# Token tiles are turned whole and kept in SBUF, with ScalarE rounding each chunk and VectorE forming its full value beside it

## The chip, the core and the metric

The kernel runs on one core of one Trainium2 chip. The metric is the time of one execution on the device in microseconds (us); the median of three runs before the change is 723.25 us (721.90 to 723.26). TensorE is also called PE, VectorE DVE, ScalarE ACT and GpSimd POOL; SyncE (SP) issues most of the DMA transfers.

## What is computed

One layer of a hybrid attention block is applied to 128 prompt tokens and 1,024 latent tokens, nine tiles of 128 tokens with 1,024 features. The part that matters here is its beginning, cut from the reference:

```python
shift, scale, gate = modulation(c, w_mod[l], b_mod[l])        # silu(c) @ w_mod + b_mod, in thirds
h = rmsnorm(xs, norm_gain[l]) * (1.0 + scale) + shift
p = h @ w_in                                                  # queries, keys, values and gates of two head groups
...
xs = xs + gate * merge_out(o_a, g_a, o_b, g_b, w_out[l])      # (o_a * silu(g_a), o_b * silu(g_b)) @ w_out
```

The prompt tokens get the same with `c_ctx` in place of `c`. So a token has to be normalized (squares summed over its features), scaled and shifted per feature, and then multiplied with the weights. Global and windowed attention, the output projection and the residual follow; the change does not touch them.

## The kernel before

**Precision.** A product of two float32 matrices is made of three TensorE products in a faster format (fp32r). Each operand is split into a rounded part (high) and the remainder (low): high x high, high x low and low x high are summed in PSUM. For the weights `Weights.split` does that (L229): ScalarE casts the high part, VectorE subtracts (`whi`, `wlo`). For the tokens it is done once in the opening stage: `h_at(0, ...)` is the high part, `h_at(1, ...)` the low one.

**Layout.** Products contract over features, so tokens must lie with the features on partitions: tile t (`xn[t]`, 128 tokens x 1,024 features) is turned in eight blocks of 128x128, one for each chunk k of 128 features, by TensorE transposes into PSUM. Scale and shift are then one number per partition (`a_mod`, `b_col`). The nine tiles stand in the order 1 to 8, then 0 (the prompt), and are cut in thirds: tiles 1 to 4 (512 columns), 5 and 6 (256), 7, 8 and 0 (384).

**The opening stage** (L333 to L502) makes `h` chunk by chunk and, at the same time, the first gate projection `W_GA` of the first two thirds. In pass j of the loop at L441:

- `W_GA.split` splits chunk j of the weights, and loads a later one;
- `first_gates(ch, j-1)` adds chunk j-1 of 512 tokens to four PSUM banks `big[0..3]`, `next_gates(ch, j-2)` that of 256 tokens to `small`;
- `modulate_rows(j)` multiplies `silu(c)` with chunk j of the modulation weights `wm` (1 MB a chunk); `modulate(j)` turns the result, and VectorE makes `a_mod` and `b_col` of chunk j from it (a reduce and two small operations, L361 to L365);
- `transposed(j, 1, 4, 0)` and `transposed(j, 5, 2, 0)` turn chunk j of four and of two tiles into a PSUM bank `px`. From there ScalarE applies scale and shift (`hf`, L401), VectorE rounds that to the high part (L406), and GpSimd subtracts for the low part (L407). From pass 5 on, `more` does the same for tiles 7, 8 and 0.

So each chunk of each tile takes the way PE, ScalarE, VectorE, GpSimd inside the pass before the one in which its products are issued.

Ahead of it, `norm(t)` (L378) makes a tile's norm: ScalarE squares and sums it (L382), GpSimd makes the inverse root (L384, L386), and VectorE scales the tile in place (`scaled`, L376). Tiles 1 to 6 are normalized in pass 0, tiles 7, 8 and 0 in passes 2 to 4. `warm` (L417) issues bfloat16 products whose result nobody reads, 24 in all before the first gate product.

**Order.** The program's order is each engine's order: `in_order` (L93) chains the instructions of an engine as they were written, and SP issues its DMAs in that order too. A tile's buffer is taken again when its last reader is done. A DMA that has to wait for a buffer holds back those behind it on SP.

After the loop `put_gates` applies silu to a bank and writes it to DRAM (scheduled for later ticks but for the first one), and `gates(W_GA, 0, W_QA, THIRDS[2:])` makes the last third. Its first PSUM bank is one of the two of `big[0]` and `big[1]`.

Of the kernel before, what the change touches and what calls it, by code (L numbers as in the profile page):

```python
# [18 lines left out]
P = 128  # L19
D = 1024  # L20
# [36 lines left out]
X_FROM = 1  # L57
SECOND_FROM = 5
WARM = (8, 4, 4, 2)
WIDE = 5  # L60
# [47 lines left out]
def hybrid_step(ctx, tc, x_prompt, x_sample, cache_k_a, cache_v_a, cache_k_b, cache_v_b,  # L108
# [97 lines left out]
    class Weights:  # L206
# [22 lines left out]
        def split(self):  # L229
# [4 lines left out]
            eng = nc.gpsimd if self.tag in POOL_LO and k % 2 else nc.vector  # L234
            eng.tensor_tensor(l, self.raw[k], h, op=ALU.subtract)
            self.hi.append(h)
            self.lo.append(l)
            self.load()
# [72 lines left out]
    with tc.tile_pool(name="st", bufs=2, side="right") as st:  # L311
# [16 lines left out]
        def load_wm(j):  # L328
            w = st.tile([P, KT, 2, P], F32, tag="wm", name=f"wm{j}", bufs=3)
            nc.sync.dma_start(w, w_mod_ss[j])  # L330
            wm.append(w)

        load_wm(0)  # L333
# [12 lines left out]
        def modulate_rows(j):  # L346
# [6 lines left out]
            (nc.scalar.copy if j else nc.vector.tensor_copy)(mrows[j], pm[:, 0:256])  # L353
# [13 lines left out]
        xn = {}  # L367
# [5 lines left out]
        rx = {}  # L373

        def scaled(t, r):
            nc.vector.tensor_scalar(xn[t], xn[t], r, None, op0=ALU.mult)  # L376

        def norm(t, now_=True):  # L378
            xm = xn[t]
            sq = st.tile([P, D], BF16, tag="sq", name=f"sq{t}", bufs=1)  # L380
            ss = st.tile([P, 1], F32, tag="ss", name=f"ss{t}")
            nc.scalar.activation(sq, xm, AF.Square, accum_out=ss)  # L382
            ms = st.tile([P, 1], F32, tag="ms", name=f"msx{t}")
            nc.gpsimd.tensor_scalar(ms, ss, 1.0 / D, EPS, op0=ALU.mult, op1=ALU.add)  # L384
            r = st.tile([P, 1], F32, tag="rs", name=f"rsx{t}")
            nc.gpsimd.tensor_tensor(r, ms, mhalf[:, 0:1], op=ALU.pow)  # L386
            if now_:
                scaled(t, r)
            else:
                rx[t] = r  # L390

        def transposed(j, t0, n, cond):
            px = bank_tr(f"px{j}_{t0}")
            for i in range(n):
                if j == 0 and t0 == 1:
                    warm(WARM[3])
                nc.tensor.transpose(px[:, P * i : P * i + P], xn[t0 + i][:, P * j : P * j + P], ident)
            w = P * n
            dst = slice(P * place(t0), P * place(t0) + w)
            hf = st.tile([P, 512], F32, tag="hf", name=f"hf{j}_{t0}", bufs=3)  # L400
            nc.scalar.activation(hf[:, :w], px[:, :w], AF.Identity,  # L401
                                 scale=a_mod[:, j, cond : cond + 1], bias=b_col[:, j, cond : cond + 1])
            step = w if third(dst) else 2 * P
            for o in range(0, w, step):
                i, to = third(slice(dst.start + o, dst.start + o + step))
                nc.vector.tensor_copy(h_at(0, i, j, to), hf[:, o : o + step])  # L406
                nc.gpsimd.tensor_tensor(h_at(1, i, j, to), hf[:, o : o + step], h_at(0, i, j, to), op=ALU.subtract)  # L407

        for t in FIRST[:4]:
            load_x(t)  # L410
        W_GA.load()
        load_x(5)
        load_x(6)
        load_wm(1)
        W_GA.load()
        load_wm(2)
        def warm(n):  # L417

            for _ in range(n):
                nc.tensor.matmul(small[0], ident_b, ident_b.unsqueeze(1).to_broadcast([P, 4, P]), start=True, stop=True)  # L420

        rest = [7, 8, 0]
        second = [(j, 7, 2, 0) for j in range(WIDE)] + [(j, 0, 1, 1) for j in range(KT)]

        big = [bank("AABB"[ch], f"pg0_{ch}_f") for ch in range(4)]
        small = [bank("C", f"pg0_{ch}_s") for ch in (0, 2)]
# [8 lines left out]
        def more():  # L435
            ready = [x for x in second if x[0] <= j]
            if ready and j >= SECOND_FROM:
                second.remove(ready[0])
                transposed(*ready[0])

        for j in range(KT + 2):  # L441
            if j == 0:
                warm(WARM[0])
                norm(1)
                modulate_rows(0)
                warm(WARM[1])
                norm(2)
                modulate(0)
                warm(WARM[2])
                norm(3)  # L450
                norm(4)
                W_GA.split()
                norm(5)
                transposed(0, 1, 4, 0)
                norm(6)
                load_wm(3)
                continue
            big_on, small_on = j <= KT, 2 <= j
            if j < KT:
                W_GA.split()  # L460
            if big_on:
                first_gates(0, j - 1, 0)
                first_gates(1, j - 1, 0)
            if j < KT:
# [3 lines left out]
                if X_FROM <= j < X_FROM + 3:  # L468
                    load_x(rest[j - X_FROM])
# [3 lines left out]
            if j == 1:  # L473
                transposed(0, 5, 2, 0)
            if big_on:
# [6 lines left out]
            if j < KT:  # L482
                transposed(j, 5, 2 if j < WIDE else 4, 0)
            if X_FROM + 1 < j <= X_FROM + 4:
                t = rest[j - X_FROM - 2]
                scaled(t, rx.pop(t))
            if X_FROM < j <= X_FROM + 3:
# [835 lines left out]
```

## Time and profile before

| | |
|---|---|
| median of three runs | 723.25 us (721.90, 723.25, 723.26) |
| span of the profiled execution | 721.3 us |
| its own time | one of the three above; 0.6 to 2.0 us lie around the span |
| mean granted TensorE clock | 0.993 |
| PE, PEld, DVE, ACT, POOL busy | 97%, 78%, 63%, 57%, 46% of the span |
| first gate product (L262) | at 17.47 us |
| second, third, fourth pass begin | at 25.30, 31.69, 37.99 us |
| first product of the last third | at 72.53 us |
| DMA | 78.56 MB in all |

The span runs from the first to the last instruction. Rows of the timeline give start and duration in us, engine, line and operation, output <- input, and in brackets how long the engine was idle before it and what released it. Rows of the windows give for a stretch its length, then each engine's busy time with the number of instructions, the granted TensorE clock (1.00 is full), the share of the DMA engines' time and GB/s. Rows of groups give the total busy time and the mean in ns.

### The profile page before, as it was taken

What the parts mean: (1) busy time and instruction counts of PE and PEld (TensorE: products, weight loads), DVE (VectorE), ACT (ScalarE), POOL (GpSimd) and SP (SyncE); (2) the same over time, 40 slices, a digit from 0 to 9 for tenths busy, and PEclk for the clock granted to TensorE, in tenths of its full rate; (3) what the DMA queues carried; (4) which work ended last, traced back from release to release, by engine and by line L of the source; (5) the groups of instructions that cost most, each with busy time, mean ns of one, the idle gap of its engine ahead of it and who ended that gap; (6) DMA issues with size and microseconds to landing.
All of it is one profiled execution on the core that took longest, in us unless ns stands there. A gap on an engine that the chain in (4) does not pass through costs nothing. (4 is left out here: it accounts for less than half of the span.)

```text
span 721.3 us, 10622 instructions
## 1 busy us (share of the span) xinstructions
PE 698.3 (97%) x3524; PEld 559.7 (78%) x3524; DVE 457.6 (63%) x1007; ACT 411.7 (57%) x829; POOL 335.3 (46%) x355
## 2 busy tenths in 40 slices
PE   5999999999999999999999999999999999999997
PEld 2678988877777788977788888888888888887865
DVE  3466147875675872745866677577666775775653
ACT  5355411411232451158778877877787778877770
POOL 3456013332322340236666555655575557555751
PEclk9999999999999999999999999999999999999999
DMA  8961373348435115440321222121212221212323
GB/s 344 346 219 59 121 278 86 79 94 276 121 85 142 45 60 171 139 143 23 103 67 45 73 67 88 44 81 52 87 54 59 66 87 45 81 53 87 103 65 119
DMA packets 53159, 78.56 MB, mean 109 GB/s; under 512 B 6569, under 2 KB 25449, under 8 KB 52081
## 3 DMA queue, kind: packets, MB, share of 16 engines
q1 hardware_dynamic: 44928, 65.96, 28.1%
q10 hardware_dynamic: 8176, 11.94, 6.3%
q8 instruction: 28, 0.46, 0.3%
q14 instruction: 27, 0.21, 0.1%
HBM read 58.69 MB, written 19.18 MB: 108 GB/s over the span
## 5 line engine op out<-in xcount | busy, mean ns | idle before, releaser
L1108 POOL TENSOR_TENSOR pl<-pe,ph 128x512 fp32r<-128x512 f32 x130 | 167.6, 1292 | 144.7 <-DVE nm L919 67.5
L859 DVE TENSOR_REDUCE mx<-pmx 128x1 f32<-128x384 f32 x192 | 101.4, 552 | 59.5 <-PE pmx L858 58.1
L1100 ACT ACTIVATE pe<-st 128x512 f32<-128x512 f32 x146 | 86.8, 594 | 28.0 <-PE st L1098 27.1
L1104 ACT CAST ph<-pe 128x512 fp32r<-128x512 f32 x146 | 90.6, 621 | 4.8
L1118 PE MATMUL pv<-ph,v_hi 128*128 128x512 f32 x208 | 83.2, 400 | 2.2 <-DVE spare L1142 2.2
L1121 PE MATMUL pv<-pl,v_hi 128*128 128x512 f32 x208 | 82.6, 397 | 0.0
L173 POOL TENSOR_TENSOR rs_q<-ms_q,mhalf 128x8 f32<-128x8 f32 x18 | 34.8, 1931 | 82.1 <-DVE ms_q L171 82.1
L1189 PE MATMUL po<-wo,ogh 128*128 128x512 f32 x216 | 72.5, 394 | 0.2 <-DVE yt L1196 0.2
L919 DVE CUSTOM_DVE_ANT_0 sn<-sn,mask,nsink 128x512 f32<-128x512 f32 (+1 forms) x64 | 46.3, 724 | 38.3 <-PE sn L916 36.5
L858 PE MATMUL pmx<-kha,qt 128*128 128x384 f32 x192 | 61.0, 363 | 0.4 <-ACT pen L905 0.2
L1097 PE MATMUL st<-qt,kha 128*128 128x512 f32 x144 | 58.3, 405 | 1.5 <-ACT pe L1100 0.8
L1098 PE MATMUL st<-qb,kla 68*128 68x512 f32 x144 | 57.6, 400 | 1.1 <-DVE qb L878 1.1
L1120 PE MATMUL pv<-ph,v_lo 128*64 128x512 f32 x146 | 57.9, 396 | 0.0
L1121 PEld LDWEIGHTS pv<-pl,v_hi 128*128 128x128 f32 x208 | 39.4, 189 | 16.7 <-issue 0.2
L905 ACT ACTIVATE pen<-sn,nm 128x512 f32<-128x512 f32 (+2 forms) x72 | 45.0, 626 | 6.5 <-DVE nm L919 3.1
L1093 ACT CAST ph<-st 128x512 fp32r<-128x512 f32 x62 | 36.4, 587 | 19.9 <-PE st L1092 18.7
L1118 PEld LDWEIGHTS pv<-ph,v_hi 128*128 128x128 f32 x208 | 39.4, 189 | 10.5 <-ACT ogh L1154 2.4
L1189 PEld LDWEIGHTS po<-wo,ogh 128*128 128x128 f32 x216 | 40.0, 188 | 6.8 <-DVE yt L1196 0.6
L1094 DVE TENSOR_TENSOR pl<-st,ph 128x512 fp32r<-128x512 f32 x62 | 42.5, 686 | 2.3 <-ACT ph L1093 1.5
L1189 PE MATMUL po<-wo,ogl 128*128 128x512 f32 x108 | 42.6, 394 | 0.0
L594 ACT ACTIVATE sqq<-pq 128x512 f32<-128x512 f32 x18 | 10.8, 599 | 53.3 <-DMA qd<-qo0q 14.4
L858 PEld LDWEIGHTS pmx<-kha,qt 128*128 128x128 f32 x192 | 35.5, 190 | 6.2 <-DVE mx L859 1.4
(216 smaller groups left out, 1700.2 us busy)
## 6 DMA issues: line engine op xcount, KB each, us to landing
qt<-qd SPq DMA_DIRECT2D x36, 256.0 KB, 3.1
wm<-in_w_mod_ss_dram SPq DMA_DIRECT2D x8, 1024.0 KB, 5.1
qd<-qo0q ACTq DMA_DIRECT2D x36, 128.0 KB, 2.4
qd<-qo1q ACTq DMA_DIRECT2D x36, 128.0 KB, 2.4
sgl<-gd SPq DMA_DIRECT2D x36, 128.0 KB, 2.1
out_dram<-yt SPq DMA_DIRECT2D x17, 256.0 KB, 2.1
xn<-in_x_sample_dram SPq DMA_DIRECT2D x8, 512.0 KB, 7.0
wg<-in_w_mod_g_dram SPq DMA_DIRECT2D x4, 1024.0 KB, 7.9
```

The source lines that it names most:

```text
L858: nc.tensor.matmul(pm[:, 0:384], lhs, kha[:, g, 3 * b : 3 * b + 3, :], start=True, stop=True)
L859: nc.vector.tensor_reduce(mx[:, h, b : b + 1], pm[:, 0:384], axis=AX.X, op=ALU.max)
L919: nc.vector.tensor_tensor_reduce(s, s, mask[:, m0 : m0 + n], -1.0, nsink[:, 4 * g + h : 4 * g + h + 1], op0=ALU.add, op1=ALU.min, accum_ou ...
L1097: nc.tensor.matmul(s, kh, qtile[i], start=True, stop=False)
L1098: nc.tensor.matmul(s, kl, qbtile[i], start=False, stop=True)
L1100: nc.scalar.activation(pe, s, AF.Exp)
L1104: nc.scalar.copy(ph, pe)
L1108: nc.gpsimd.tensor_tensor(pl, pe, ph, op=ALU.subtract)
L1118: nc.tensor.matmul(pv, two, ph, start=(b == 0), stop=False)
L1120: nc.tensor.matmul(pv[0:64, :], vl, ph, start=False, stop=False)
L1121: nc.tensor.matmul(pv, two, pl, start=False, stop=last)
L1189: nc.tensor.matmul(po[n], a, wo_parts[KT * n + k][lo], start=(k == KS[0] and p == 0), stop=(k == KS[-1] and p == 2))
```

## The change

The opening stage is written in another way; nothing else changes.

- **Loads.** Tiles 1 to 4 come first on SP's queue, then `wm0` in two halves, then the first weight chunk, tile 5, `wm1`, tile 6, and so on. Before, `wm0` came first. Token tiles share four buffers, so the load of tile 5 waits until tile 1 is turned, 6 for 2, 7 for 3, 8 for 4, 0 for 5.
- **Turning.** `turned_tile(t)` turns all eight blocks of a tile into two banks, and `keep` copies them from PSUM to a new SBUF tile `xT` (1,024 features x 1,152 tokens), one bank by ScalarE and one by VectorE. Tiles 1 to 4 are turned before the first gate product, 5 in pass 1, 6 in pass 2, and 7, 8, 0 in passes 3, 4, 5.
- **Modulating.** `modulated` reads `xT`: ScalarE writes the high part straight from it (scale, shift and rounding in one), VectorE makes the full value `hf` from the same input, and GpSimd subtracts as before. The high part of a chunk no longer goes through VectorE.
- **Squares.** The squares of tiles 1 to 4 stand first in ScalarE's queue; those of 5 to 0 are spread over the passes.
- Warm products: 8 at the start and 4 before the first gate product. The low part of the first weight chunk is made by GpSimd. `mrows` of chunk 1 is copied by VectorE. The first `put_gates` stands before the last pass, and `sg` has two buffers of its own (before it shared three with `hf`). `more` starts at the same pass, but makes up to four pieces a pass.

```diff
-WARM = (8, 4, 4, 2)
-WIDE = 5
+WARM = (8, 4)
...
-        load_wm(0)
         nc.scalar.activation(silc, colt[:, 0:16], AF.Silu)
...
-            (nc.scalar.copy if j else nc.vector.tensor_copy)(mrows[j], pm[:, 0:256])
+            (nc.scalar.copy if j > 1 else nc.vector.tensor_copy)(mrows[j], pm[:, 0:256])
...
+        xT = st.tile([P, KT, TOK], F32, name="xT", bufs=1)
 
         def load_x(t):
-            xn[t] = st.tile([P, D], F32, name=f"xn{t}", bufs=1)
+            xn[t] = st.tile([P, D], F32, tag="xn", name=f"xn{t}", bufs=4)
             nc.sync.dma_start(xn[t], x_tile[t])
...
+        def turned_tile(t, tags, between=None):
+
+            for c in range(2):
+                if c and between:
+                    between()
+                px[t, c] = bank(tags[c], f"px{t}_{c}")
+                for i in range(4):
+                    k = 4 * c + i
+                    nc.tensor.transpose(px[t, c][:, P * i : P * i + P], xn[t][:, P * k : P * k + P], ident)
+
+        def keep(t, c, copy):
+            at = slice(P * place(t), P * place(t) + P)
+            copy(xT[:, 4 * c : 4 * c + 4, at], px.pop((t, c)).rearrange("p (k n) -> p k n", n=P))
+
+        def modulated(j, t0, n, cond):
...
+            a, b = (x[:, j, cond : cond + 1] for x in (a_mod, b_col))
             hf = st.tile([P, 512], F32, tag="hf", name=f"hf{j}_{t0}", bufs=3)
-            nc.scalar.activation(hf[:, :w], px[:, :w], AF.Identity,
-                                 scale=a_mod[:, j, cond : cond + 1], bias=b_col[:, j, cond : cond + 1])
-            step = w if third(dst) else 2 * P
-            for o in range(0, w, step):
-                i, to = third(slice(dst.start + o, dst.start + o + step))
-                nc.vector.tensor_copy(h_at(0, i, j, to), hf[:, o : o + step])
-                nc.gpsimd.tensor_tensor(h_at(1, i, j, to), hf[:, o : o + step], h_at(0, i, j, to), op=ALU.subtract)
+            nc.scalar.activation(h_at(0, i, j, to), xT[:, j, dst], AF.Identity, scale=a, bias=b)
+            nc.vector.tensor_scalar(hf[:, :w], xT[:, j, dst], a, b, op0=ALU.mult, op1=ALU.add)
+            nc.gpsimd.tensor_tensor(h_at(1, i, j, to), hf[:, :w], h_at(0, i, j, to), op=ALU.subtract)
...
+        for t in (1, 2, 3, 4):
+            squares(t)
+        warm(WARM[0])
+        for t, tags in ((1, "AB"), (2, "AB"), (3, "CC")):
+            scaled(t)
+            turned_tile(t, tags)
+            if t > 1:
+                for c in range(2):
+                    keep(t - 1, c, copies[c])
+        scaled(4)
+        modulate_rows(0)
+        keep(3, 0, copies[0])
+        W_GA.split(nc.gpsimd)
+        turned_tile(4, "AB", lambda: modulate(0))
+        keep(4, 0, copies[0])
+        modulated(0, 1, 4, 0)
+        keep(3, 1, copies[1])
+        keep(4, 1, copies[1])
+        load_wm(3)
+        load_x(0)
+        squares(5)
+        warm(WARM[1])
...
+            if j == KT + 1:
+                put_gates(big[0], 0, 0, slice(0, 512))
...
+            if j in rest:
+                scaled(rest[j])
+            if j + 1 in rest:
+                squares(rest[j + 1])
...
             if j < KT:
                 modulate(j)
-                transposed(j, 1, 4, 0)
+                if j == 1:
+                    W_GA.split()
+                modulated(j, 1, 4, 0)
+                if j == 1:
+                    scaled(6)
...
+            if j in rest:
+                turned_tile(rest[j], "DE")
+                for c in range(2):
+                    keep(rest[j], c, copies[c])
...
-        sg_tile.append(lambda n: st.tile([P, 512], F32, tag="hf", name=n, bufs=3))
-        put_gates(big[0], 0, 0, slice(0, 512))
```

The order of the instructions at three places on which the prediction rests. In each, `xn` are token tiles, `wm` modulation weights, `rawga` weights as loaded; the trailing numbers tell buffers apart.

SyncE's queue at the start, before:

```order
L330 DMA wm_169<-in_w_mod_ss_dram 128x2048
L371 DMA xn_178<-in_x_sample_dram 128x1024
L371 DMA xn_180<-in_x_sample_dram 128x1024
L371 DMA xn_182<-in_x_sample_dram 128x1024
L371 DMA xn_184<-in_x_sample_dram 128x1024
L221 DMA rawga_186<-in_w_in_dram 128x512
L371 DMA xn_188<-in_x_sample_dram 128x1024
L371 DMA xn_190<-in_x_sample_dram 128x1024
L330 DMA wm_192<-in_w_mod_ss_dram 128x2048
L221 DMA rawga_194<-in_w_in_dram 128x512
```

and with the change:

```order
L370 DMA xn_177<-in_x_sample_dram 128x1024
L370 DMA xn_179<-in_x_sample_dram 128x1024
L370 DMA xn_181<-in_x_sample_dram 128x1024
L370 DMA xn_183<-in_x_sample_dram 128x1024
L329 DMA wm_185<-in_w_mod_ss_dram 128x1024 x2
L219 DMA rawga_188<-in_w_in_dram 128x512
L370 DMA xn_190<-in_x_sample_dram 128x1024
L329 DMA wm_192<-in_w_mod_ss_dram 128x2048
L370 DMA xn_194<-in_x_sample_dram 128x1024
L219 DMA rawga_196<-in_w_in_dram 128x512
```

The four tiles moved past `wm0`, and `wm1` past tile 6; tile 5 (`xn_190`) takes the buffer of tile 1.

TensorE just before its first gate products, before (`px` is the bank with chunk 0 of four tiles, `pg` the gate banks):

```order
L397 MATMUL px_1_283<-ident,xn_182 128x128
L420 LDWEIGHTS ident_b
L420 MATMUL pg_0_s<-ident_b 128x512
L420 LDWEIGHTS ident_b
L420 MATMUL pg_0_s<-ident_b 128x512
L397 MATMUL px_1_283<-ident,xn_184 128x128
L262 MATMUL pg_0_f<-h_0_0_115,whiga_269 128x512
L263 MATMUL pg_0_f<-h_0_0_115,wloga_270 128x512
```

and with the change, ahead of the four warm products and the first gate products (`pm` is the bank of the modulation's rows):

```order
L392 MATMUL px_1_260<-ident,xn_179 128x128 x4
L392 MATMUL px_0_268<-ident,xn_181 128x128 x4
L392 MATMUL px_1_273<-ident,xn_181 128x128 x4
L348 MATMUL pm_281<-wm_185,sil_173 32x256 x8
L392 MATMUL px_0_299<-ident,xn_183 128x128 x4
L357 MATMUL pm_281<-ident,mrows_290 128x128 x2
L392 MATMUL px_1_310<-ident,xn_183 128x128 x4
```

A tile's eight blocks now stand together, 32 of them before the first gate product instead of 4, and the rows of chunk 0 come behind the third tile.

VectorE in pass 3, before:

```order
L235 TENSOR_TENSOR wloga_447<-rawga_314,whiga_446 128x512
L361 TENSOR_REDUCE m_3_478<-pm_456 128x4
L363 TENSOR_SCALAR a_mod<-m_3_478,bsc_172,colt 128x2
L365 TENSOR_SCALAR b_col<-m_3_478,colt 128x2
L406 CAST h_0_3_118<-hf_1_487 128x512
L406 CAST h_1_2_132<-hf_5_497 128x256
L376 TENSOR_SCALAR xn_333<-xn_333,rsx_432 128x1024
L235 TENSOR_TENSOR wloga_522<-rawga_376,whiga_521 128x512
```

and with the change:

```order
L233 TENSOR_TENSOR wloga_491<-rawga_297,whiga_490 128x512
L382 TENSOR_SCALAR xn_202<-xn_202,rsx_454 128x1024
L359 TENSOR_REDUCE m_3_528<-pm_500 128x4
L361 TENSOR_SCALAR a_mod<-m_3_528,bsc_170,colt 128x2
L363 TENSOR_SCALAR b_col<-m_3_528,colt 128x2
L406 TENSOR_SCALAR hf_1_532<-xT,a_mod,b_col 128x512
L396 COPY xT<-px_1_544 128x4x128
L406 TENSOR_SCALAR hf_5_551<-xT,a_mod,b_col 128x256
L233 TENSOR_TENSOR wloga_568<-rawga_382,whiga_567 128x512
```

The scale of tile 7 moved in front of the reduce, the rounding of h gave way to `hf`, and a copy out of PSUM came in between.

More of the change, by code (lines that the diff above doesn't have):

```diff
@@ L392, in transposed, with scaled @@
[L392 to L397, printed above, removed]
+            rx[t] = st.tile([P, 1], F32, tag="rs", name=f"rsx{t}", bufs=4)
+            nc.gpsimd.tensor_tensor(rx[t], ms, mhalf[:, 0:1], op=ALU.pow)
+        def scaled(t):
+            nc.vector.tensor_scalar(xn[t], xn[t], rx.pop(t), None, op0=ALU.mult)
@@ L422, in hybrid_step @@
[L422 to L426, printed above, removed]
+                nc.tensor.matmul(idle, ident_b, ident_b.unsqueeze(1).to_broadcast([P, 4, P]), start=True, stop=True)
+        second = [x for k in range(KT) for x in ((k, 7, 2, 0), (k, 0, 1, 1))]
         def first_gates(ch, k, part=None):
@@ L491, in hybrid_step @@
                     next_gates(ch, j - 2)
-                if ch % 2 or j >= KT:
+                if j > SECOND_FROM or (j == SECOND_FROM and ch % 2):
                     more()
```

95 lines of the change are left out of this document (40 added, 55 removed).

## The prediction

> **What bounds the kernel now.** I read the page's engine line first, then the windows of the passes of the opening stage, then the timeline of the first 18 us.
>
> ```profile
> PE 698.3 (97%) x3524; PEld 559.7 (78%) x3524; DVE 457.6 (63%) x1007; ACT 411.7 (57%) x829; POOL 335.3 (46%) x355
> ```
>
> TensorE is the bound of the whole; what it does not do before it starts, or does not have to do between products, shortens the run. The change touches only the stage up to the first product of the last token third. I cut that stage at the first product of each pass j (windows: length, then busy time of PE, PEld, DVE, ACT, POOL, granted clock, DMA share, GB/s):
>
> ```profile
> 17.47:25.30 7.83, 7.13 (x39) 4.43 (x39) 2.68 (x7) 2.72 (x6) 2.75 (x4) 0.78 1.02 421
> 25.30:31.69 6.39, 6.39 (x48) 4.91 (x49) 3.11 (x7) 2.89 (x6) 2.86 (x3) 1.00 0.92 333
> 31.69:37.99 6.30, 6.30 (x51) 4.82 (x50) 2.67 (x7) 3.16 (x7) 3.16 (x5) 1.00 0.82 293
> 37.99:44.28 6.29, 6.29 (x50) 4.81 (x49) 4.16 (x8) 3.15 (x7) 3.60 (x5) 1.00 0.77 289
> 44.28:51.14 6.86, 6.86 (x56) 5.38 (x55) 4.36 (x7) 3.20 (x7) 4.17 (x5) 1.00 0.62 194
> 51.14:58.08 6.94, 6.94 (x57) 5.46 (x56) 5.73 (x11) 3.77 (x7) 4.89 (x6) 1.00 0.49 152
> 58.08:64.93 6.85, 6.85 (x57) 5.36 (x55) 5.03 (x10) 3.49 (x6) 4.67 (x6) 1.00 0.01 3
> 64.93:72.53 7.60, 6.67 (x46) 5.93 (x44) 4.34 (x11) 4.27 (x10) 5.72 (x12) 1.00 0.00 0
> ```
>
> From pass 2 (25.30) to pass 7 PE is busy throughout: there a pass costs what PE has to do in it. Pass 1 and the last row hold stalls, and before 17.47 there is no product at all. What sets 17.47, with DMA beside it (the last two windows are looked at under the clock):
>
> ```profile
> 5.00:10.00 5.00, 4.76 (x25) 1.37 (x23) 0.00 (x0) 1.85 (x3) 0.68 (x2) 1.00 1.01 415
> 10.00:15.00 5.00, 3.38 (x17) 1.69 (x17) 3.56 (x8) 4.41 (x9) 3.57 (x8) 1.00 1.04 426
> 15.53:18.94 3.41, 1.61 (x13) 0.93 (x16) 1.45 (x3) 2.43 (x4) 2.12 (x3) 1.00 1.02 423
> 18.94:22.36 3.42, 3.42 (x22) 2.02 (x15) 1.35 (x2) 0.86 (x2) 0.68 (x2) 0.50 1.02 422
> ```
>
> ```profile
> 6.86 1.94 PE L350 MATMUL pm<-wm,sil 128*32 128x256 f32 x16
> 8.00 1.06 ACT L382 ACTIVATE sq<-xn 128x1024 bf16<-128x1024 f32 x1 [4.51 <-DMA xn<-in_x_sample_dram]
> 11.79 1.06 ACT L382 ACTIVATE sq<-xn 128x1024 bf16<-128x1024 f32 x1
> 14.54 0.75 DVE L376 TENSOR_SCALAR xn<-xn,rsx 128x1024 f32<-128x1024 f32 x1 [0.71 <-POOL rsx L386]
> 15.35 0.33 PE L397 MATMUL px<-ident,xn 128*128 128x128 f32 x1 [0.70 <-DVE xn L376]
> 15.71 0.78 ACT L401 ACTIVATE hf<-px,b_col,a_mod 128x512 f32<-128x512 f32 x1 [0.86 <-PE px L397]
> 17.00 0.42 DVE L406 CAST h<-hf 128x512 fp32r<-128x512 f32 x1
> 17.47 0.50 PE L262 MATMUL pg_f<-h,whiga 128*128 128x512 f32 x1 [1.80 <-DVE h L406]
> ```
>
> DMA is full (415 and 426 GB/s). The modulation weights of chunk 0 come first, so their rows are done by 8.8, and the token tiles come last: the first square starts at 8.00, the fourth at 11.79, and the chain square, scale, transpose, hf, rounding ends at 17.47.
>
> **First product.** With the four tiles ahead of wm0, tile 1 lands 1.05 MB / 0.42 MB per us = 2.5 us earlier, about 5.5, and each further tile 0.52/0.42 = 1.25 later: the fourth by 9.3. From the fourth square's start to its scale are 14.54-11.79 = 2.75 us, so tile 4 is scaled by 12.8. It is no longer last. The last is wm0: 9.3+2.5 = 11.8. From there the chain is rows, copy of the rows, two transposes, reduce, a_mod, b_col, then ScalarE's h0:
>
> ```profile
> 26.42 1.07 PE L350 MATMUL pm<-wm,sil 128*32 128x256 f32 x16
> 3.33 3.60 PE L420 MATMUL pg_s<-ident_b 128*128 128x512 bf16 x8 [3.33 <-DVE ident_b L315]
> 8.72 1.04 PE L420 MATMUL pg_s<-ident_b 128*128 128x512 bf16 x4
> 10.79 0.42 DVE L353 COPY mrows<-pm 128x256 f32<-128x256 f32 x1
> 11.26 0.44 PE L359 MATMUL pm<-ident,mrows 128*128 128x128 f32 x2 [1.50 <-DVE mrows L353]
> 41.76 0.17 DVE L361 TENSOR_REDUCE m<-pm 128x4 f32<-128x16 f32 x1 [1.14 <-PE pm L359]
> 42.51 1.23 ACT L401 ACTIVATE hf<-px,b_col,a_mod 128x512 f32<-128x512 f32 x2 [1.99 <-DVE b_col L365]
> ```
>
> 11.8 + 1.07 + 0.5 + 0.5 + 0.75 (41.76 to 42.51) + 0.78 + two hand-overs of 0.1 = 15.6 with PE at full speed. The first warm products took 3.60/8 = 0.45 us each, the next 1.04/4 = 0.26, and the rows 1.94 at 6.86 against 1.07 later: PE starts near half speed although the clock column says 1.00. If it still runs so, the rows cost 0.9 more, the transposes and the four warm products in front of the first product about 1.5: 18.0. I take 16.6, -0.9 against 17.47. The DVE rounding (0.42) leaves this path, because ScalarE writes h0 itself; chunk 0's weight remainder on GpSimd needs ga0, the next transfer, and has until 16.
>
> The x5 load now waits for tile 1 to be turned and holds wm1, x6, ga1 and wm2 behind it on SP's queue. Tile 1 is turned near 9.7, while the engines have bytes until (2.2+1.05+0.26)/0.42+3.3 = 11.7, so nothing runs dry; wm1 lands near 16, its rows are due near 17.5.
>
> **Transposes out of the passes.** The line's share of the passes (PE busy and count first):
>
> ```profile
> 31.69:37.99 6.30, 0.98 (x6) 0.75 (x6) 1.00 0.82 293
> 44.28:51.14 6.86, 1.71 (x12) 1.45 (x12) 1.00 0.62 194
> ```
>
> Six more lengthen a full pass by 6.86-6.30 = 0.56: about 0.1 us each; a pass without any is 5.7. Before, 4 of the 72 precede the first product; now 32 do (tiles 1 to 4 whole), and tiles 5, 6, 7, 8, 0 put 8 each into passes 1 to 5. So passes 3, 4, 5 become 6.5 (+0.2, +0.2, -0.35), 6 and 7 5.7 (-1.25, -1.15).
>
> In the last row PE is busy 6.67 of 7.60, 8 transposes among it:
>
> ```profile
> 72.53 0.44 PE L262 MATMUL pg<-h,whiga 128*128 128x384 f32 x1 [0.94 <-ACT sg L289]
> ```
>
> The 0.94 us wait is for the bank that the first put_gates empties; that now stands in front of pass 9. So 5.9, -1.7.
>
> **Passes 1 and 2.** Pass 1 has no small products:
>
> ```profile
> 30.18 0.36 PE L262 MATMUL pg_s<-h,whiga 128*128 128x256 f32 x1
> 31.69 0.40 PE L262 MATMUL pg_f<-h,whiga 128*128 128x512 f32 x1
> ```
>
> These take 31.69-30.18 = 1.5, so its work is 5.7-1.5+0.8 = 5.0 where it took 7.83, of which 3.42 us at clock 0.50 (the window from 18.94). I take 5.4: -2.4. Pass 2 gets tile 6 whole, in front of its rows, behind scaled(6), which VectorE reaches only after wlo and hf of pass 1: 5.7+0.8+0.7 = 7.2, +0.8.
>
> **What is added, and its cover.**
>
> ```profile
> L1093 ACT CAST ph<-st 128x512 fp32r<-128x512 f32 x62 | 36.4, 587 | 19.9 <-PE st L1092 18.7
> L1094 DVE TENSOR_TENSOR pl<-st,ph 128x512 fp32r<-128x512 f32 x62 | 42.5, 686 | 2.3 <-ACT ph L1093 1.5
> 37.69 1.79 DVE L376 TENSOR_SCALAR xn<-xn,rsx 128x1024 f32<-128x1024 f32 x1
> 39.40 1.22 DVE L235 TENSOR_TENSOR wloga<-rawga,whiga 128x512 fp32r<-128x512 f32 x1
> ```
>
> Nine copies out of PSUM on ScalarE, 9 x 0.587 = 5.3 us, nine on VectorE, 9 x 0.686 = 6.2 us at most: one of each per pass, where ScalarE is busy 3.2 of 6.3 and VectorE 4.2. At nothing, while that slack holds. The hf that VectorE now makes from SBUF isn't in the trace: between the cast's 0.42 and the stretched 1.2; off h0's path, it only feeds GpSimd's remainder, used a third of a pass later. What has little cover is the chain to the next h0: the reduce starts 41.76-37.99 = 3.8 into a pass, ScalarE 0.75 later, 0.78 long: 5.35 of 5.7. I charge 0.3 to each of passes 6 and 7.
>
> Sum: -0.9 -2.4 +0.8 +0.05 -2.4 -1.7 +0.6 = -6.0 us. The profiled span is 721.3; 723.25, the median of the three runs, lies 1.95 above it, and I take that as what lies around the span: 715.3 + 1.95 = 717.2. What follows 72.53 waits for its own predecessors and moves along.
>
> **Rivals.**
> *The clock.* In 15.53:18.94 PE was busy 1.61 of 3.41 us, and the next 3.42 us were granted 0.50. Warm products fall from 24 to 12, and what fills the start is transposes with gaps. If these do not hold the clock, the first product comes at 18.0 (+1.4) and a half-speed window falls into pass 1 (+1.7): 720.3. For: that window; against: four warm products stand right in front of the first product, and the products themselves follow without gaps. The Trainium skill, "TensorE: Matmul & The Clock Gate", Part 4 (PE-mode transpose), says that transposes do not count as a busy PE for the gate; its Part 1 sets the gate by windows of about 3.4 us, which the 3.42 us agrees with. By that rule this rival is the case; before mixes transposes with warm products, so its trace cannot tell. Chance 0.12.
>
> *VectorE's order, slower.* Now scaled(7), 1.79 us (0.75 at 14.54), and pass 4's wlo, 1.22, both long beside a busy GpSimd, end 1.14 before the reduce is due. With the change scaled(t) stands directly in front of the reduce in passes 3 to 5, behind wlo, and the copies and up to six hf of a pass queue there too. Each us by which the reduce starts later than the 0.35 to 1.15 of slack is a us of PE, in each of seven passes. Above 1.1 us each, the 6.0 us are gone and 1.5 more: from reduces that start 1.5 to 2.2 us later than 3.8 into the pass, 725.0. For: 5.73 us busy in pass 6; against: that held a scale of its own. Chance 0.07.
>
> *Given back.* The later stages wait for the same thing as before, at an absolute time (a load that isn't pulled forward): 723.2. Against: between 72.53 and the next stage's loads PE waits for nothing. Chance 0.05.
>
> **How the numbers follow.** Forecast 0.76, the rivals 0.12, 0.07, 0.05. Two per mille, 1.45 us, is about what a measurement of this kernel tells from no change: faster 0.88, same 0.05, slower 0.07. The early end: first product at 15.6 (-1.9), pass 1 5.0 (-2.8), no stall in pass 2 (+0.1), 6 and 7 free: -8.6, 714.6. The late end takes in the clock: 720.5.
>
> **What would show it.** First product at 15.6 to 18.0; the first wait in front of it for ScalarE's h0, not for a scaled tile; passes 6 and 7 at 5.7 to 6.0 with PE full; no 0.94 us wait in front of L260's last third; the rest as long as before. Wrong, if the PE windows of passes 3 to 7 hold waits for ScalarE or VectorE, or the clock is 0.50 beyond 19 us.

## The result, and the profile after

The changed kernel takes 716.66 us (median of four runs, 715.88 to 717.18) against 723.25 us (721.90 to 723.29) before: a ratio of 0.9907, 95% interval 0.9893 to 0.9921, or 6.6 us. The profiled executions differ by 6.1 us: spans of 715.2 and 721.3. The forecast was 717.2.

The windows of the changed kernel, cut as before at the first product of each pass (the last one ends at the first product of the last third):

```profile
17.16:22.51 5.35, 5.34 (x38) 3.62 (x38) 3.49 (x9) 3.52 (x7) 3.10 (x5) 1.00 1.03 409
22.51:29.11 6.60, 6.60 (x51) 5.22 (x51) 5.22 (x12) 5.12 (x10) 4.28 (x6) 1.00 1.03 416
29.11:35.63 6.52, 6.52 (x53) 5.03 (x52) 4.41 (x8) 4.13 (x9) 4.08 (x5) 1.00 1.03 412
35.63:42.15 6.52, 6.52 (x53) 5.03 (x52) 4.46 (x9) 3.73 (x8) 3.17 (x5) 1.00 0.91 326
42.15:48.66 6.51, 6.51 (x53) 5.02 (x51) 4.45 (x9) 2.66 (x6) 2.42 (x3) 1.00 0.52 167
48.66:54.29 5.63, 5.63 (x45) 4.19 (x44) 4.13 (x10) 2.66 (x6) 2.74 (x5) 1.00 0.43 130
54.29:59.91 5.62, 5.62 (x44) 4.16 (x43) 5.48 (x11) 3.54 (x9) 4.48 (x6) 1.00 0.19 70
59.91:66.08 6.17, 6.00 (x39) 5.13 (x37) 6.17 (x10) 5.73 (x13) 6.16 (x9) 1.00 0.11 42
```

The second number of a row is PE's busy time. It now fills every pass up to the last row, which has 0.17 us of stall where it had 0.93 (7.60 less 6.67).

| stretch | before | forecast | after |
|---|---|---|---|
| first product | 17.47 | 16.6 | 17.16 |
| pass 1 | 7.83 | 5.4 | 5.35 |
| pass 2 | 6.39 | 7.2 | 6.60 |
| passes 3, 4, 5 | 6.30, 6.29, 6.86 | 6.5 each | 6.52, 6.52, 6.51 |
| pass 6 | 6.94 | 6.0 | 5.63 |
| pass 7 | 6.85 | 6.0 | 5.62 |
| last row | 7.60 | 5.9 | 6.17 |
| first product of the last third | 72.53 | 66.5 | 66.08 |

The start, in PE's timeline (bracket: idle time before the row and what ended it), and the window in which the clock was halved:

```profile
8.66 1.09 PE L392 MATMUL px<-ident,xn 128*128 128x128 f32 x8 [1.97 <-DVE xn L382]
10.17 3.38 PE L392 MATMUL px<-ident,xn 128*128 128x128 f32 x16 [0.42 <-DVE xn L382]
13.48 1.07 PE L348 MATMUL pm<-wm,sil 128*32 128x256 f32 x16
17.16 0.50 PE L260 MATMUL pg_f<-h,whiga 128*128 128x512 f32 x1 [0.33 <-ACT h L405]
```

```profile
9.80:13.00 3.20, 2.83 (x14) 2.83 (x14) 2.49 (x5) 2.22 (x4) 2.06 (x4) 0.50 1.01 373
```

Eight transposes took 1.09 us at 8.66; the next sixteen took 3.38 instead of 2.2, at clock 0.50. Before the change such a window lay in pass 1. What PE waits for in the first 80 us (total, times, longest):

```profile
PE idle L426 <- DVE ident_b L313: 3.4, 1, 3.4
PE px L392 <- DVE xn L382: 2.4, 2, 2.0
PE pg_f L260 <- ACT h L405: 0.3, 1, 0.3
PE pg_f L256 <- POOL h L407: 0.2, 1, 0.2
```

After the first product one wait of 0.2 us is left. The copies and `hf` found their cover: VectorE makes the twelve last `hf` back to back, and the one wait of 0.2 us, for GpSimd's h that is made from them, is all that PE pays after its first product.

```profile
59.09 7.61 DVE L406 TENSOR_SCALAR hf<-xT,a_mod,b_col 128x512 f32<-128x512 f32 x12
```

### The profile page after: what moved, and what is told of

Its sections match the earlier page's. It is cut to its first block, busy times and chain, and to the rows that moved or that the text cites. A ratio compares the mean times of both kernels' runs of the same rounds, so it can differ in the third digit from the quotient of the medians.

```text
span 715.2 us, 10633 instructions
## 1 busy us (share of the span) xinstructions
PE 694.4 (97%) x3512; PEld 559.1 (78%) x3512; DVE 463.8 (65%) x1016; ACT 416.4 (58%) x840; POOL 334.6 (47%) x356
## 3 DMA queue, kind: packets, MB, share of 16 engines
HBM read 58.69 MB, written 19.18 MB: 109 GB/s over the span
```

## The experiments

"Passes 7 to 9" means pass 7 and the last row: 14.45 us before (13.52 of it busy), 11.79 after (11.62).

**The start: more warm products, and the order of the loads.** First, 12 products instead of 8:

```diff
-WARM = (8, 4)
+WARM = (12, 4)
```

> The changed kernel with 12 warm products at the start in place of 8. Theory: in the changed kernel PE is idle from 6.7 to 8.66 us, the clock falls to 0.50 from 9.7 to 13.1, and the turning of tiles 2 and 3 at half speed holds back the rows of chunk 0 by about 1 us. Four more products end near 8.3; the clock stays full, the first gate product moves from 17.16 to 16.1 to 16.5, all passes last as long as before, and the time falls by 0.7 to 1.0 us to about 715.8. Rival (the start is bound by the arrival of wm0 or tile 4, whatever the clock): first product at 17.1, 716.7.

Measured: 715.92 us (715.13 to 716.38), ratio 0.9899 (0.9884 to 0.9913). PE's timeline of its start:

```profile
3.42 5.05 PE L426 MATMUL idle<-ident_b 128*128 128x512 bf16 x12 [3.42 <-DVE ident_b L313]
9.67 1.09 PE L392 MATMUL px<-ident,xn 128*128 128x128 f32 x8 [0.32 <-DVE xn L382]
11.36 1.09 PE L392 MATMUL px<-ident,xn 128*128 128x128 f32 x8 [0.60 <-DVE xn L382]
12.38 1.07 PE L348 MATMUL pm<-wm,sil 128*32 128x256 f32 x16
16.50 0.50 PE L260 MATMUL pg_f<-h,whiga 128*128 128x512 f32 x1 [0.76 <-ACT h L405]
```

All transposes run at full speed, the rows start 1.1 us earlier and the first product 0.66 earlier, at 16.50. Tile 1 was scaled 0.7 us earlier in this execution, but that is not the reason: the kernel with more transposes (below) has its tile 3 scaled when the change has it (10.84 and 10.83), turns it at full speed, and starts its rows at 12.67, 0.8 us before the change. So half speed was what cost the first-product term. The rows gain more than the first product, because `a_mod` took 0.72 us here instead of 0.29 (see the last experiment). The time is 0.7 us less, and the intervals of the two ratios overlap: the trace shows the gain, the times alone don't.

Second, the modulation weights first again, ahead of the token tiles:

```diff
+        load_wm(0)
         for t in (1, 2, 3, 4):
             load_x(t)
-        load_wm(0)
```

> The changed kernel with wm0 in front of the four token tiles on the queue, as before the change. Theory: the order of the loads sets only the first gate product. Tile 4 lands 2.5 us later, near 12.2, its square, scale, turning, copy out of PSUM and h0 follow, and the first product comes at 17.9 to 18.5 in place of 17.16; passes 2 to 7 stay as they are (6.6, 6.5, 6.5, 6.5, 5.6, 5.6): slower by 0.8 to 1.3 us, about 717.7. Rival (the loads in this order are where the gain comes from): most of the 6.6 us is lost, 720 or more.

Measured: 720.20 us (720.00 to 721.66), ratio 0.9963 (0.9950 to 0.9976). PE's timeline:

```profile
11.75 4.92 PE L392 MATMUL px<-ident,xn 128*128 128x128 f32 x24 [4.90 <-DVE xn L382]
16.60 1.07 PE L348 MATMUL pm<-wm,sil 128*32 128x256 f32 x16
20.29 0.50 PE L260 MATMUL pg_f<-h,whiga 128*128 128x512 f32 x1 [0.33 <-ACT h L405]
```

All passes keep their length; the whole cost is in front of them, 3.1 us. That is about half of the gain; the rival said most of it, and the time lies just in its range. The theory had the place right and the size too small. The first squares of this kernel and of the changed one show why:

```profile
8.83 1.06 ACT L375 ACTIVATE sq<-xn 128x1024 bf16<-128x1024 f32 x1 [5.74 <-DMA xn<-in_x_sample_dram]
```

```profile
5.74 1.06 ACT L375 ACTIVATE sq<-xn 128x1024 bf16<-128x1024 f32 x1 [2.37 <-DMA xn<-in_x_sample_dram]
```

Tile 1 comes 3.1 us later, and there is no slack behind it: the rows, which wait for no weights now, stand behind the 24 transposes on PE and start 3.1 us later too (16.60 for 13.48), and so does the first product. Half speed is no part of the difference as far as can be seen, since both starts have it: here PE had been idle for 4.9 us, and most of the 24 transposes took 0.42 us each instead of 0.27. With whole tiles turned ahead of the rows, the tiles have to come first.

**The squares first.** Each square directly ahead of its tile's scale:

```diff
-        for t in (1, 2, 3, 4):
-            squares(t)
         warm(WARM[0])
         for t, tags in ((1, "AB"), (2, "AB"), (3, "CC")):
+            squares(t)
             scaled(t)
...
+        squares(4)
         scaled(4)
```

> The changed kernel with the squares of tiles 1 to 4 no longer first in ScalarE's queue: each stands directly ahead of its tile's scale, so the copies out of PSUM of tiles 1 and 2 stand ahead of the squares of tiles 3 and 4. Theory (the order of ScalarE's queue sets when tiles 3 and 4 are scaled, and with them the rows and the last turning): the third square starts near 9.9 instead of 8.51, the fourth near 11.7 instead of 9.79, chunk 0's rows and the turning of tile 4 move by about 1 us, first product near 18.1 instead of 17.16 (16.75 to 16.79 where the start runs at full clock), time 717.5 to 717.9. Rival (the rows wait for their weights, and the turning has slack): first product 16.7 to 17.2, time 716.4 to 716.8.

Measured: 716.24 us (715.93 to 717.76), ratio 0.9895 (0.9874 to 0.9915). ScalarE's timeline:

```profile
4.93 1.06 ACT L375 ACTIVATE sq<-xn 128x1024 bf16<-128x1024 f32 x1 [1.53 <-DMA xn<-in_x_sample_dram]
...
8.55 0.59 ACT L396 COPY xT<-px 128x512 f32<-128x512 f32 x1 [0.33 <-PE px L392]
9.03 1.06 ACT L375 ACTIVATE sq<-xn 128x1024 bf16<-128x1024 f32 x1
...
11.17 1.06 ACT L375 ACTIVATE sq<-xn 128x1024 bf16<-128x1024 f32 x1
```

The copies do stand in front of the squares, and the fourth square starts at 11.17 instead of 9.79. The first product came at 17.55, 0.39 later than with the change and between the two forecasts, and the passes were the same; the time cannot be told from the change's. The expected microsecond was too much, in part because tile 1 landed earlier in this execution (its square at 4.93 instead of 5.74). The clock column says 0.50 from 11 to 13 us in this start as well, so one pair of profiles cannot give the price closely. Squares first is worth some tenths here, no more.

**The rounding.** Back on VectorE, from SBUF:

```diff
-            nc.scalar.activation(h_at(0, i, j, to), xT[:, j, dst], AF.Identity, scale=a, bias=b)
-            nc.vector.tensor_scalar(hf[:, :w], xT[:, j, dst], a, b, op0=ALU.mult, op1=ALU.add)
+            nc.scalar.activation(hf[:, :w], xT[:, j, dst], AF.Identity, scale=a, bias=b)
+            nc.vector.tensor_copy(h_at(0, i, j, to), hf[:, :w])
```

> The changed kernel with the rounding back on VectorE: ScalarE writes hf from xT, VectorE casts it to the high part, GpSimd subtracts as before. Theory: the chain to h0 grows by a cast and a hand-over, 0.5 us. That shows at the first product (17.16 to 17.7) and in the passes without a turned tile, 6 and 7 (5.63 to about 5.9), not in passes 3 to 5 (6.52): slower by 0.8 to 1.5 us, about 717.8. Rival A (ScalarE's rounding is the source of the gain): 720 or more. Rival B (it is worth nothing): 716.7 and pass 6 at 5.6.

Measured: 720.52 us (719.21 to 721.15), ratio 0.9961 (0.9946 to 0.9976): 3.9 us slower than the change, in the range of rival A and not of the theory. In the profiles the last third begins at 68.77 instead of 66.08, so the stage shows 2.7 us of it; the one execution of this kernel with a granted clock of 1.000 has a span of 717.2 us, 2.7 above the mean of the change's at that clock (below). Pass 1 takes 5.78 and pass 2 6.83 us; pass 6, pass 7 and the last row together take 5.83 + 13.35 = 19.18 against 5.63 + 11.79 = 17.42 with the change (the next expectation calls these three "passes 7 to 9"). ScalarE's timeline late in the stage, and PE's beside it:

```profile
56.90 0.49 ACT L405 ACTIVATE hf<-xT,b_col,a_mod 128x128 f32<-128x128 f32 x1 [1.01 <-POOL h L407]
57.64 1.19 ACT L405 ACTIVATE hf<-xT,b_col,a_mod 128x256 f32<-128x256 f32 x2 [0.25 <-POOL h L407]
58.74 0.60 ACT L231 CAST whiga<-rawga 128x512 fp32r<-128x512 f32 x1
59.25 0.36 ACT L351 COPY mrows<-pm 128x256 f32<-128x256 f32 x1
...
68.14 0.58 ACT L287 ACTIVATE sg<-pg_f 128x512 f32<-128x512 f32 x1
```

```profile
59.67 0.44 PE L357 MATMUL pm<-ident,mrows 128*128 128x128 f32 x2 [0.69 <-ACT mrows L351]
```

ScalarE works in order. When it makes `hf`, it needs one of three buffers, and GpSimd frees them. It stands 1.01 us for one, so the copy of the rows behind it is late and PE waits 0.69 us for it; the first silu, at 68.14, is late too, though the last third hardly waits for it. The price of the longer chain to h0 was expected (from the rows to the first product 4.23 us instead of 3.68; 0.4, 0.2 and 0.2 us in passes 1, 2 and 6); this was not. One more buffer shows how much of it the buffers are:

```diff
-            hf = st.tile([P, 512], F32, tag="hf", name=f"hf{j}_{t0}", bufs=3)
+            hf = st.tile([P, 512], F32, tag="hf", name=f"hf{j}_{t0}", bufs=4)
```

> The changed kernel with the rounding back on VectorE (ScalarE makes hf, VectorE casts it, GpSimd subtracts), and with four hf buffers instead of three. With three it took 720.52 us, 3.9 more than the change, and ScalarE stood before hf buffers that GpSimd frees. Theory (those buffers tie ScalarE to GpSimd): one more buffer gives back a part, passes 7 to 9 shrink from 19.2 us to 17.8-18.5, time 719.0 to 719.8. Rival (the longer chain through VectorE costs by itself): passes and time as with three buffers, 720.5.

Measured: 719.61 us (719.13 to 720.94), ratio 0.9957 (0.9943 to 0.9972), in the expected range of the time. The three stretches took 5.83 + 12.88 = 18.71 us where 18.5 at most was expected: 0.47 of the 1.76 came back. What ScalarE and PE still wait for:

```profile
62.90 1.24 ACT L405 ACTIVATE hf<-xT,b_col,a_mod 128x256 f32<-128x256 f32 x2 [0.62 <-POOL h L407]
```

```profile
61.42 0.50 PE L260 MATMUL pg_f<-h,whiga 128*128 128x512 f32 x1 [0.45 <-DVE h L406]
```

So both theories hold in part: the buffers cost, and so does the longer chain, of which PE waits 0.45 us for VectorE's h. How the rest divides stays open.

**The price of a transpose.** `modulate`'s two transposes issued three times, with the same data:

```diff
-            for s in range(2):
+            for s in (0, 1) * 3:
```

> The changed kernel with the two transposes of each modulate issued three times, so four more transposes in each of passes 1 to 7 and four ahead of the first product. Theory: a transpose in a pass costs 0.1 us of PE. 28 more cost 2.8 us and the four ahead about 0.4: passes 6 and 7 go from 5.63 to about 6.0, 3 to 5 from 6.52 to about 6.9, slower by 2.6 to 3.4 us, about 719.7. Rival (the passes are bound by ScalarE, VectorE or GpSimd, so that transposes are hidden and their removal was not the gain): passes as long as they are, 716.7 to 717.1.

Measured: 719.71 us (718.85 to 720.30), ratio 0.9955 (0.9938 to 0.9971). Passes 4 and 6:

```profile
36.58:43.51 6.93, 6.93 (x57) 5.46 (x55) 4.46 (x9) 3.70 (x8) 3.14 (x5) 1.00 0.76 267
50.45:56.52 6.07, 6.07 (x48) 4.64 (x47) 4.14 (x10) 2.68 (x6) 2.75 (x5) 1.00 0.47 150
```

Against 6.52 and 5.63 that is 0.41 and 0.44 for four transposes: 0.1 us each, in a full pass and in one without a tile. Taking transposes out of the passes pays at just that rate.

**The clock in the kernel before.** Six warm products more, after the last norm:

```diff
+                warm(6)
```

> The kernel before with six more warm products after the last norm of pass 0, in front of chunk 0's last transposes, where PE was idle between 15.7 and 17.5 us. Theory (pass 1's loss before the change was the half-speed window 18.94 to 22.36, set off by that idle time): the window goes from pass 1, which takes about 6.1 us instead of 7.83; time about 721.6 us (-1.6). Rival (pass 1 was long because of what its engines had to do, or the window falls as it likes): pass 1 stays between 7.5 and 7.9 and the time at 723.2.

Measured: 722.18 us (721.36 to 724.63), ratio 0.9993 (0.9980 to 1.0006): no difference that can be told. Its pass 1, a window further on, and pass 1 of the kernel before with another edit (the next experiment) that leaves the start alone:

```profile
17.54:24.20 6.66, 5.77 (x38) 3.50 (x38) 2.98 (x7) 2.81 (x6) 2.75 (x4) 1.00 1.03 422
...
320.00:325.00 5.00, 5.00 (x13) 3.82 (x14) 1.38 (x3) 4.16 (x10) 3.19 (x4) 0.50 0.44 151
```

```profile
17.46:24.13 6.67, 5.77 (x39) 3.52 (x39) 2.97 (x7) 2.82 (x6) 2.75 (x4) 1.00 1.02 420
```

With the products pass 1 runs at full clock and takes 6.66, but without them it can do so too, 6.67. So the window of the first profile, 7.83 - 6.67 = 1.16 us, belonged to that execution and not to every one. The kernel before, as it is or with edits further on that leave its start alone, was profiled four times here: twice the window lies in pass 1, and twice it does not. The longest is that of the early silu with six buffers (below):

```profile
17.51:26.61 9.10, 8.42 (x38) 5.07 (x38) 2.67 (x7) 2.75 (x6) 2.75 (x4) 0.65 1.01 412
```

The theory's 1.6 us for every execution do not stand. Whether the products keep the window away where it would have come, one profile with them cannot tell.

**The first gate output.** In the kernel before, moved ahead of the last pass; and in the changed one, moved back behind the loop:

```diff
+            if j == KT + 1:
+                sg_tile.append(lambda n: st.tile([P, 512], F32, tag="hf", name=n, bufs=3))
+                put_gates(big[0], 0, 0, slice(0, 512))
...
-        put_gates(big[0], 0, 0, slice(0, 512))
```

> The kernel before with the first gate output put ahead of the last pass, as the change does it, and nothing else. Theory (the 0.94 us wait in front of the last third was the late silu of that bank): the wait goes, first product of the last third at 71.6 instead of 72.53, time 722.3 us (-0.9). Rival (ScalarE, which works in order, stands before a buffer that GpSimd has to free, so the silu runs no earlier): the wait stays over 0.5 us and the time is 723.0 to 723.3.

> The changed kernel with the first gate output back behind the loop; its buffers of its own stay. Theory (ScalarE is done early with its work of the last passes, so the place of the silu costs only its own length and the hand-over): the wait in front of the last third comes back with 0.5 to 0.9 us, time 717.1 to 717.6. Rival (VectorE's or GpSimd's last pieces set the end of the loop, so the bank is not what is waited for): no wait, 716.7.

Measured: the first 723.01 us (721.77 to 726.10), ratio 1.0009 (0.9995 to 1.0022); the second 716.62 us (715.36 to 717.28), ratio 0.9911 (0.9895 to 0.9928), the change's own. The kernel before with the move, ScalarE and PE:

```profile
69.23 0.60 ACT L289 ACTIVATE sg<-pg_f 128x512 f32<-128x512 f32 x1
```

```profile
70.84 0.33 PE L397 MATMUL px<-ident,xn 128*128 128x128 f32 x1 [0.91 <-ACT hf L401]
```

and passes 7 to 9 of the changed kernel without it:

```profile
54.27:66.07 11.80, 11.63 (x80) 9.28 (x79) 11.65 (x19) 9.29 (x21) 10.65 (x15) 1.00 0.08 30
```

The early silu takes its wait away and puts another of the same size in its place: ScalarE does the silu instead of the next `hf`, whose bank `px` PE needs. Passes 7 to 9 stay at 14.45. In the changed kernel the late silu costs nothing (11.80 against 11.79), where the theory expected 0.5 to 0.9 us: no wait for it stands in front of the last third. The place of this step is worth nothing in either kernel.

**Before, with more buffers.** Six `hf` buffers in the kernel before, alone and together with the early silu:

```diff
-            hf = st.tile([P, 512], F32, tag="hf", name=f"hf{j}_{t0}", bufs=3)
+            hf = st.tile([P, 512], F32, tag="hf", name=f"hf{j}_{t0}", bufs=6)
```

> The kernel before with six hf buffers instead of three, nothing else. Theory (ScalarE stands before hf buffers that GpSimd frees): its waits for GpSimd in passes 7 to 9 go; the first silu comes up to 0.4 us earlier, so passes 7 to 9 take 14.0 to 14.3 us instead of 14.45, time 722.4 to 722.7 against 722.8. Rival (the buffers are free in time where it matters): 14.45 and 722.8.

> The kernel before with the first gate output ahead of the last pass and six hf buffers, so both at once; the first alone left passes 7 to 9 at 14.45 us, with a wait of 0.91 us for ScalarE's hf in place of that of 0.94 for the silu. Theory (the early silu and GpSimd's buffers together make the wait): with both changes it goes, passes 7 to 9 take 13.5 us, time 721.9 (-0.9). Rival (the last row is bound by the chain PE, ScalarE, VectorE, GpSimd of its own pieces): 14.3 to 14.45 us, time 722.5 to 723.0.

Measured: 722.82 us (721.24 to 723.97), ratio 0.9996 (0.9985 to 1.0008), and 721.72 us (721.24 to 724.97), ratio 0.9984 (0.9975 to 0.9994). Passes 7 to 9, buffers alone, then both, and PE's wait in the latter:

```profile
57.13:71.37 14.24, 13.49 (x100) 11.29 (x98) 9.18 (x20) 7.73 (x15) 10.34 (x17) 1.00 0.00 1
```

```profile
59.40:73.69 14.29, 13.54 (x99) 11.34 (x98) 8.91 (x19) 7.23 (x15) 9.65 (x15) 1.00 0.05 18
```

```profile
73.17 0.33 PE L397 MATMUL px<-ident,xn 128*128 128x128 f32 x1 [0.75 <-ACT hf L401]
```

The buffers are worth 0.2 us, within what their theory allowed, and the two together no more; 0.75 us of stall stay. The theory of the two causes falls, the rival holds: by the wait that is left, the last row was bound by the way PE, `px`, ScalarE. No run here gives `px` another bank, which would test it. The second kernel's time is lower by 1.2 us, of which its stage shows 0.2; six of its eleven executions ran at a granted clock of 1.000, against four of 21 of the kernel before, so the time says little about the edit.

**A faster version.** The 12 products, and the low part of the first weight chunk on VectorE:

```diff
-WARM = (8, 4)
+WARM = (12, 4)
...
-        W_GA.split(nc.gpsimd)
         turned_tile(4, "AB", lambda: modulate(0))
+        W_GA.split()
```

> The changed kernel with 12 instead of 8 warm products at the start, and the low part of the first weight chunk on VectorE behind chunk 0's small operations instead of on GpSimd beside them. Theory (what is left in front of the first product is the chain of the modulation's small operations, of which a_mod took 0.72 us beside GpSimd instead of 0.29): a_mod is back at 0.3, first product at 16.1 (16.50 with the 12 products alone), time 715.5, which would be the fastest kernel here. Rival (the split stands in VectorE's way of hf, so the first product's partner comes later): first product earlier but the second waits by as much, time 715.9.

Measured: 716.34 us (715.79 to 717.25), ratio 0.9908 (0.9892 to 0.9923). The two rows of VectorE, without and with the move (of the 12 products alone, and of this kernel), and this kernel's PE and ScalarE:

```profile
14.69 0.72 DVE L361 TENSOR_SCALAR a_mod<-m,bsc,colt 128x2 f32<-128x2 f32 x1
```

```profile
14.52 0.29 DVE L361 TENSOR_SCALAR a_mod<-m,bsc,colt 128x2 f32<-128x2 f32 x1
```

```profile
15.89 0.50 PE L260 MATMUL pg_f<-h,whiga 128*128 128x512 f32 x1 [0.33 <-ACT h L405]
...
26.20 0.44 PE L357 MATMUL pm<-ident,mrows 128*128 128x128 f32 x2 [0.37 <-ACT mrows L351]
```

```profile
23.66 0.62 ACT L231 CAST whiga<-rawga 128x512 fp32r<-128x512 f32 x1 [1.83 <-DMA rawga<-in_w_in_dram]
```

The first product comes 0.61 us earlier than with the 12 products alone, as the theory said, but pass 1 takes 5.52 and pass 2 7.20 (5.34 and 6.60 there), and the last third starts at 65.65 instead of 65.39. The gain is given back, at another place than the rival named: ScalarE stands 1.83 us before a weight chunk that has not landed, the copy of the rows is queued behind it, and PE waits for that. The kernel with the late silu shows the same, smaller: its start at 16.75 was 0.41 us earlier than the change's, its pass 2 took 6.91 instead of 6.60, and its last third began at 66.07, where the change's did. An earlier start pays only as far as that load lets it, and the load does not land alike in every execution: with the 12 products alone ScalarE stood 1.11 us before the same chunk, had it at 23.37, and pass 2 lost nothing, while the kernel with the late silu started later and had it at 24.06. No version here beats the change by more than the measurement tells.

## Why the prediction was right, step by step

- **First product, -0.9: measured -0.3, mis-sized.** The chain had `wm0` as the last thing to arrive, at 11.8. In the change's execution the rows waited for the turning instead, whose sixteen last transposes fill PE from 10.17 to 13.48 at clock 0.50; the value taken lay near "PE at full speed". With 12 warm products the term is -0.97 (16.50), and there turning and weights end nearly together: the loading of PE's weights for the rows waits 0.27 us for `wm0`, until 12.81, a microsecond later than forecast. That the value taken fits the kernel with these products is in part luck. In the kernel with the late silu, whose start is the change's own, the first product came at 16.75, with sixteen slow transposes as well, but earlier ones.
- **Pass 1, -2.4: measured -2.48, the size right, the reason partly.** Of it, 1.16 us was the half-speed window of that one execution (7.83 against 6.67); 0.90 was stall (6.67 - 5.77 busy), of which 0.53 is a wait for the h that VectorE rounded, and with the rounding back on VectorE a wait of 0.46 returns; 0.43 was work that left (5.77 - 5.34). The prediction named the clock and reckoned the work that stays; it had no term for the stall.
- **Pass 2, +0.8: measured +0.21, mis-sized.** The stall of 0.7 us before tile 6 did not come: the pass is busy for 6.60 of 6.60. A stall does come where the next weight chunk lands late for the start: 7.20 in the last experiment, there for the rows queued behind that chunk.
- **Passes 3 to 5: +0.22, +0.23, -0.35**, as forecast to 0.03 us; the price of 0.1 us a transpose was measured by itself.
- **Passes 6 and 7, -1.8 together: measured -2.54 (5.63 and 5.62 against 6.0).** The floor of 5.7 was right, the 0.3 us charged to each for thin cover were not needed: PE is busy throughout.
- **Last row, -1.7: measured -1.43, the size nearly right, the cause in the step wrong.** The step put 0.94 us down to the place of the silu. That place is worth nothing in either kernel. Passes 7 to 9 lost 13.52 - 11.62 = 1.9 us of PE work and 0.76 us of stall; that the stall went because ScalarE no longer reads PSUM banks that PE waits for is argued from the waits, not tried by itself. The rounding put back shows the other part: ScalarE before the buffers that GpSimd frees.
- **The rounding.** Its 0.42 us on the way to h0 was one of its uses; the other, freeing ScalarE from GpSimd's pace, was not in the prediction, and one more buffer gives 0.47 us of it back. Undone by itself the rounding costs 2.7 us in the stage and 3.9 in the time. The load order undone costs 3.1: together that is more than the 5.3 us that the change gains without the clock (below), so the prices of undoing are no parts of one sum.
- **The rivals.** *The clock* came true in part: a half-speed window, but while tiles were turned, where it cost about 0.7 us of the first product (16.50 without it), and not in pass 1. *VectorE's order* did not come: no wait of PE in the passes stands behind a reduce. *Given back*: from the first product of the last third to the end the two profiles take 648.8 and 649.1 us. In two profiles with 1.000 in the clock column, the kernel before with the early silu and the changed one with the late, this tail is 719.8 - 71.36 = 648.4 and 714.6 - 66.07 = 648.5. So nothing is given back; the 0.3 us are not the stage's.

So the total came within 0.6 us in part by luck: the first product and pass 2 miss by 0.6 us each in opposite ways, and 1.16 us of pass 1 came from one execution of the kernel before.

The two profiles at 1.000 also give the gain without the clock, as far as its column tells: 5.3 us at the first product of the last third. Of the executions beside the experiments, the 16 of the kernel before with a granted clock of 0.999 or more have a mean span of 720.0 us, and the five of the change and of its late-silu version at 1.000 one of 714.5: 5.5 us. The 6.1 and 6.6 us of the comparison hold 0.6 to 1.1 more; in the profiles that is the window in pass 1. The kernel before had that clock in 16 of 58 executions, the change and its late-silu version 1.000 in five of eight. Part of the loss lies outside the stage: twelve of the fourteen profiles, of both kernels, hold another stretch of clock 0.50 between 311 and 326 us, and the two without it are those with 1.000. Why was not tried.

## What to carry to other kernels

Engines that work in order pass on each other's waits through buffers: before moving a late step forward, ask what the engine would then not do, for a wait that ends on a silu can come back on the copy behind it. Turning data ahead and keeping it paid by the transposes that left the full passes, 0.1 us each, and, as far as the waits tell, by the PSUM banks that no engine has to hand back in time. And read the profile of one execution together with its clock: a half-speed window may belong to the execution and not to the kernel.

## What the runs showed of the hardware

**Transposes bring the clock back.** In the changed kernel the half-speed window from 9.8 to 13 us holds nothing but transposes on PE, and the rows at 13.48 run at full speed (1.07 us). With the weights first, PE comes out of 4.9 us of idling, does 24 transposes, the first at 0.42 us and the last at 0.27 each, and then the rows at 1.07:

```profile
L392 PE MATMUL px<-ident,xn x24: 272/421/474, 11.8 to 16.4; 128*128 128x128 f32 x24
```

(minimum, median and maximum of their duration in ns). The prediction's rival leaned on the Trainium skill, "TensorE: Matmul & The Clock Gate", Part 4 (PE-mode transpose), by which transposes do not count as a busy PE; these runs disagree with it, as far as a MATMUL row tells that it is such a transpose. Part 1 of the same page of the Trainium skill says that the window runs freely, so that the same kernel warms up at different times; that agrees with the start of the change, which had its slow stretch from 9.8 us in one execution and, in one of the kernel with the late silu and the same start, from 8.15.

**The clock column misses a cold start.** In that other execution sixteen transposes took 3.44 us, most of them 0.417 us each, while the column says 1.00:

```profile
8.15:11.59 3.44, 3.44 (x16) 3.20 (x16) 1.80 (x3) 2.31 (x5) 1.30 (x3) 1.00 1.00 348
```

It says 1.00 over the 24 transposes of the kernel with the weights first as well. There the duration of a known operation tells the speed, not the column.
